# The closing order of two output projections, one W_out piece in another ring, and the memory projections' banks

## The chip, the cores and the metric

The kernel runs on one core of a Trainium2 chip. The metric is the device time of one execution in microseconds, here the median of several runs. TensorE does the matrix products and writes them to PSUM; VectorE, ScalarE and GpSimd (POOL) work on SBUF, the first two also on PSUM; SyncE issues the transfers.

## The reference

A trunk of two layers on x of 1024 tokens by 1024 channels, with 256 memory tokens. In each layer:

```python
h = x @ w_in                      # columns: main | memory queries | main gate | memory gate
y_main = main_fn(u_main)          # layer 0: causal pooling; layer 1: forgetting attention, 16 heads
y_mem  = memory_attention(q_mem, mem, w_mem_kv)      # 4 heads of 128 over 256 memory tokens
y = concat([y_main * silu(g_main), y_mem * silu(g_mem)]) @ w_out     # 1536 x 1024
x = layer_norm(ALPHA * x + y, ln_g, ln_b)
```

Memory attention first makes keys and values of the memory tokens: `mem @ w_mem_kv`, four heads of each. All of it is in float32.

## The kernel before, in words

**Products in three parts.** A float32 operand is split into a high half (a cast on ScalarE, L187) and a low half (a subtract on VectorE, or on POOL for some weights, L188, L198). One product of float32 numbers becomes three on TensorE (`three`, L217): high by high ("large", f32 in the profile) and two with a low half ("small", bf16). `grouped` (L222) puts the large ones ahead of the small ones, or behind them when it is `turned`.

**Slots.** Tiles come from rings by tag: `T` has 6 slots, `w` and `wl` 4 each (high and low halves of weights), `raw` 4 (weights as they arrive), `MK`, `Y`, `P`, `G` 4 each. A tile takes a slot of its tag that is free at that point of the compiled order, and its first writer waits for the last reader of what was there. PSUM's banks are tagged as well: `pj` 2, `L` 3, `T` 2, `O` 1. TensorE's instructions keep the order of the program (`manual_schedule`). Those of the other engines are put in order when the kernel is compiled, by what is ready and, among that, by the program's order; each engine then takes its queue in that order.

**Output projection** (`OutProj`, L432). The tokens go in four pairs of token tiles (sp = 0 to 3, two tiles `a` of 128 tokens). Each pair has four banks, `accs[a][nh]`, one for each token tile and half of the columns. The rows of W_out go in three chunks `c` of 512 rows, four row tiles `k` each, in the order c = 2, 0, 1. A chunk is 48 products of 512 columns (2 token tiles x 2 halves x 4 row tiles x 3). `products` (L474) issues them: all 16 large ones, then all 32 small ones (for c = 0 the other way round), each in the order token tile, half, row tile. So all four banks of a pair stay open into the small products of c = 1. For each chunk `rest` (L500) loads `src` and splits it (`hi_lo`, L517), which takes three slots of `T`: source, high, low.

**Norm** (L527). After c = 1 each token tile is normalised on VectorE: L537 takes up a bank (alpha times x plus the product), L538 its statistics, twice; L540 to L546 make the mean and the reciprocal root (with one square root on ScalarE, L542); L548 and L550 are the two passes over the 1024 columns, in halves for the very last tile; then the tile is stored (L551). In layer 0 the normalised tiles are also transposed on TensorE (L348) for layer 1; those of the last pair are put between layer 1's memory projections (L361).

**W_out.** Its 12 pieces (256 rows by 512 columns) are split ahead of use into whatever slots are free; `wtags` (L651 for layer 0) names the tag of each. Pieces 0 to 3 serve chunk 2, 4 to 7 chunk 0, 8 to 11 chunk 1; even ones are the first half of the columns. A piece in the weights' ring takes 2 slots of `w` and all 4 of `wl`.

**Memory keys and values** (`mem_kv`, L286). The memory rows are split into four tiles of `T`. `project` (L298) makes one head's keys or values: 24 products of 256 columns into a `pj` bank, with two pieces of weights (one low half on POOL and one on VectorE in layer 1). Keys are split from the bank into `MK` (L315); values are scaled first (`scaled_halves`, L327: a reduction and five short instructions on VectorE, then L339 on ScalarE and L340 on VectorE read the bank). In layer 0 keys and values of a head follow its queries (L364 to L370); in layer 1 all eight projections come first, keys then values, with the two transposes between, and then the queries' products (`slab`, L253, also into `pj`).

Of the kernel before, what the change touches and what calls it, by code (L numbers as in the profile page):

```python
# [18 lines left out]
P = 128  # L19
# [3 lines left out]
ST = S // P  # L23
NH = 512
HEADS = 16
MH = 4
NMEM = 256
# [72 lines left out]
def trunk_kernel(ctx, tc, x, xT, memT, win, wk, wv0, wv, wmk, wmv, wout, poolw, pscale, lng, lnb, bforget, out):  # L100
# [21 lines left out]
    def nm(tag):  # L122
        count[0] += 1
        return f"{tag}{count[0]}"

    def sb(shape, tag, bufs, dt=F32, where=None):
        return (where or pool).tile(shape, dt, tag=tag, name=nm(tag), bufs=bufs)

    def ps(shape, tag, bufs):
        return psum.tile(shape, F32, tag=tag, name=nm(tag), bufs=bufs)  # L130
# [4 lines left out]
    def T(shape=(P, S), dt=F32R):  # L135
        return sb(list(shape), "T", 6, dt)

    def MK(shape, dt=F32R):
        return sb(list(shape), "MK", 4, dt)

    def raw(shape):
        return sb(list(shape), "raw", 4)
# [8 lines left out]
    def cut(pair, *key):  # L151

        return type(pair)(t[key] for t in pair)

    def halved(make, shape):

        return make(list(shape)), duo(make([shape[0], 2, *shape[1:]], BF16))

    def in_place(make, shape):

        hi = make(list(shape))
        return hi, InPlace((make(list(shape), BF16), hi.bitcast(BF16)[..., 1::2]))
# [21 lines left out]
    def hi_lo(hi, lo, src, pinned=False, aside=False, by=nc.vector):  # L184

        pin = tc.keep_in_program_order if pinned else lambda ins: ins
        pin(nc.scalar.copy(hi, src))  # L187
        pin(by.tensor_tensor(lo[0], src, hi.bitcast(F32), ALU.subtract))  # L188
        if isinstance(lo, InPlace):
            return  # L190
        if pinned or aside:
            nc.gpsimd.tensor_scalar(lo[1], hi.bitcast(F32), 1.0, 1.0, ALU.mult, ALU.mult)  # L192
        else:
            nc.scalar.copy(lo[1], hi.bitcast(F32))
# [5 lines left out]
    def split_w(src_dram, shape, by=nc.vector):  # L200
        r = raw(shape)
        nc.sync.dma_start(r, src_dram)
        h, l = in_place(wt, shape)
        gp_hi_lo(h, l, r) if low[0] else hi_lo(h, l, r, by=by)
        return h, l
# [11 lines left out]
    def three(a, b):  # L217

        (ah, al), (bh, bl) = a, b
        return (ah, bh), (al[1], bl[0]), (al[0], bl[1])  # L220

    def grouped(triples, turned=False):  # L222


        large, small_ = [t[0] for t in triples], [m for t in triples for m in t[1:]]
        return small_ + large if turned else large + small_

    def mm3(acc, terms):

        for i, (a, b) in enumerate(terms):  # L230
            nc.tensor.matmul(acc, a, b, start=i == 0, stop=i == len(terms) - 1)  # L231
# [54 lines left out]
    def mem_kv(l):  # L286

        mh, ml = zip(*(halved(T, [P, 4, NMEM]) for _ in range(2)))
        for q in range(4):
            r = raw([P, 2, NMEM])  # L290
            nc.sync.dma_start(r, memT[:, 2 * q : 2 * q + 2, :])
            two = slice(2 * (q % 2), 2 * (q % 2) + 2)
            hi_lo(mh[q // 2][:, two, :], cut(ml[q // 2], slice(None), two), r)
        kh, kl = halved(MK, [P, MH, NMEM])

        turned = [False]

        def project(w_dram):  # L298

            acc = ps([P, NH], "pj", 2)[:, :NMEM]  # L300
            terms = []
            for pc in range(2):
                a, b = split_w(w_dram[pc], [P, 4, P], nc.gpsimd if l and not pc else nc.vector)
                terms += [
                    three((a[:, k, :], cut(b, slice(None), k)), (mh[pc][:, k, :], cut(ml[pc], slice(None), k))) for k in range(4)
                ]
            turned[0] = not turned[0]
            mm3(acc, grouped(terms, turned[0]))
            return acc

        two, v = (MK([P, MH, 2 * 2, P], F16) for _ in range(2))
        undo = const.tile([P, 8], F32, tag="undo", name=nm("undo"), bufs=1)[:, :MH]

        def keys(h):
            hi_lo(kh[:, h, :], cut(kl, slice(None), h), project(wmk[l, h]))  # L315

        def vals(h):
            scaled_halves(
                project(wmv[l, h]), [two[:, h, 2 * e : 2 * e + 2, :].rearrange("p m t -> p (m t)") for e in range(2)],
                undo[:, h : h + 1],  # L320
            )
            if h == MH - 1:
                nc.sync.dma_start_transpose(v.rearrange("p h b d -> p (h b) d"), two.rearrange("p h b t -> p (h b t)"))

        return (kh, kl, v, undo), keys, vals

    def scaled_halves(u, halves, un, by_tile=lambda t: t):  # L327

        m, e, sc = (tiny(1) for _ in range(3))
        nc.vector.tensor_reduce(m, u, AX.X, ALU.max, apply_absolute_value=True)
        nc.vector.tensor_scalar(m, m, 2.0 ** -100, None, ALU.max)
        nc.vector.tensor_scalar(e.bitcast(I32), m.bitcast(I32), 0x7F800000, None, ALU.bitwise_and)
        nc.vector.reciprocal(sc, e)
        nc.vector.tensor_scalar(sc, sc, 2.0 ** 14, None, ALU.mult)
        nc.vector.tensor_scalar(un, e, 2.0 ** -15 / PSCALE, None, ALU.mult)
        (hi, lo), u = halves, by_tile(u)
        nc.scalar.activation(hi, u, AF.Copy, scale=sc)  # L339
        nc.vector.scalar_tensor_tensor(lo, u, sc, hi, ALU.mult, ALU.subtract)  # L340
# [91 lines left out]
    class OutProj:  # L432
# [38 lines left out]
            accs = [ps([P, NH], *bank) for bank in turned[sp % len(turned)]]  # L471
            return accs[:2], accs[2:]

        def products(self, accs, c, yh, yl):  # L474
            terms = []
            for a in range(2):
                rows = slice(a * P, (a + 1) * P)
                for nh in range(2):
                    for k in range(4):
                        kt = 4 * c + k  # L480
                        w = tuple(part[kt % 2] for part in self.ws[nh][kt // 2])
                        terms.append([(accs[a][nh], x) for x in three((yh[:, k, rows], cut(yl, slice(None), k, rows)), w)])
            order = grouped(terms, c == 0)
            firsts, lasts = ({id(acc): j for j, (acc, _) in way} for way in (reversed(list(enumerate(order))), enumerate(order)))
            for j, (acc, (y, w)) in enumerate(order):
                nc.tensor.matmul(acc, y, w, start=c == 2 and j == firsts[id(acc)], stop=c == 1 and j == lasts[id(acc)])  # L486
                yield NH
# [12 lines left out]
        def rest(self, resid, XH, XL, dst):  # L500
            self.split(24)
            gb = []
            for v in (lng, lnb):
                t = sb([P, D], "P", 4)
                nc.sync.dma_start(t, v[self.l].partition_broadcast(P))
                gb.append(t)
            accs, turns = {}, []
            if self.accs:
                accs[0], order = self.accs, [(0, 0), (1, 2), (0, 1), (1, 0), (1, 1)]
            else:  # L510
                order = [(sp, c) for sp in range(2) for c in (2, 0, 1)]
            for sp, c in order + [(sp, c) for sp in range(2, ST // 2) for c in (2, 0, 1)]:
                if c == 2:
                    accs[sp] = self.open(sp)
                src, (yh, yl) = T([P, 4, 2 * P], F32), in_place(T, [P, 4, 2 * P])
                nc.sync.dma_start(src, self.yd[c, :, :, sp * 2 * P : (sp + 1) * 2 * P])
                hi_lo(yh, yl, src)  # L517
                for n, _ in enumerate(self.products(accs[sp], c, yh, yl)):
                    at = (sp, ((2, 0, 1).index(c) * 48 + n))
                    while turns and turns[0][0] <= at:  # L520
                        turns.pop(0)[1]()
                if c == 1:
                    made = norm(sp, accs.pop(sp), gb, resid, XH, XL, dst)
                    turns += [((sp + 1, n), turn) for n, turn in zip((44, 84), made)]
            return [turn for _, turn in turns]
# [66 lines left out]
    with tc.tile_pool(name="in0", bufs=1) as in0:  # L592
# [55 lines left out]
                    nc.vector.scalar_tensor_tensor(yn, acc, pschalf[:, f : f + 1], yn, ALU.mult, ALU.mult)  # L648
                nc.sync.dma_start(y0d[f // 4, :, f % 4, :], ys[d])

        wtags = [("B", 8)] * 4 + [("W", 4)] * 2 + [("MK", 4)] * 2 + [("Y", 4)] * 2 + [("PG", 0), ("w", 0)]  # L651
        out_proj = OutProj(0, w_slots(wtags, in0), y0d)
        order = ExitStack()
        order.enter_context(tc.manual_schedule(engines={PE}))
# [13 lines left out]
    with tc.tile_pool(name="in1", bufs=1) as in1:  # L668
# [390 lines left out]
        wtags = [("B", 10), ("V", 4), ("MK", 4)] + [("B", 10)] * 3 + [("w", 0), ("MK", 4), ("R", 2), ("V", 4), ("PG", 0), ("B", 10)]  # L1059
# [69 lines left out]
```

## Time and profile before

| | |
|---|---|
| median of 3 runs | 1225.47 us (1223.59 to 1226.15) |
| the profiled execution | 1221.52 us, its span 1219.8 us |
| TensorE busy | 1187.1 us, 97% of the span |
| VectorE, ScalarE, POOL busy | 786.8, 607.5, 201.7 us |
| granted TensorE clock, mean | 0.997 |
| layer 0's last product (L486) to the queries' first of layer 1 (L253) | about 461 to 489.76 us |
| last product of layer 1 starts | 1208.63 us |

Lines of the timeline give start and length in us, engine, line, operation, what is written and read, and how many were merged; in brackets the idle time of the engine before it and what ended it. A line of the waits gives the total, the number and the longest. A product's end is modelled: 0.27 us after its start for 256 columns and 0.38 for 512, while the next may start sooner. Names such as `wl` or `L` are the tags above. The share of busy time hardly tells anything here; what counts is where TensorE stands still.

### The profile page before, as it was taken

How to read it: one execution, taken by the hardware profiler on the slowest of the kernel's cores; microseconds unless marked ns; L12 is line 12 of the kernel's file. 1: busy time of each engine (PE TensorE's matmuls, PEld its weight loads, DVE VectorE, ACT ScalarE, POOL GpSimd, SP SyncE). 2: the span in 40 equal slices, each digit the busy share in tenths (PEclk: the TensorE clock that was granted, in tenths of full speed). 3: DMA queues.
4: the chain of work that ended last, by engine and by line, in shares of the span. 5: the costliest groups of instructions: out<-in, count | busy, mean ns of one | idle time of the engine just before them, and what ended most of it. 6: DMA issues, size and time to landing. Idle time of an engine off the chain costs nothing. (4 is left out here: it accounts for less than half of the span.)

```text
span 1219.8 us, 19568 instructions
## 1 busy us (share of the span) xinstructions
PE 1187.1 (97%) x6903; PEld 749.7 (61%) x7018; DVE 786.8 (64%) x1861; ACT 607.5 (50%) x1318; POOL 201.7 (17%) x312
## 2 busy tenths in 40 slices
PE   9999999999999998999999999999999999999996
PEld 4567665555556567557776666666666666655553
DVE  6544776375554459247645878777878878775653
ACT  6433654263431134257434777767766777673110
POOL 2000000000000004000003334333334324530000
PEclk9999999999999999999999999999999999999998
DMA  6332454242363325224618688769797999985430
GB/s 233 114 105 90 125 113 156 79 130 89 119 207 111 113 104 174 87 59 107 183 50 176 162 186 174 193 154 184 176 190 175 174 200 212 226 232 187 167 109 35
DMA packets 267410, 178.65 MB, mean 146 GB/s; under 512 B 212272, under 2 KB 225712, under 8 KB 267312
## 3 DMA queue, kind: packets, MB, share of 16 engines
q1 hardware_dynamic: 267312, 177.40, 55.5%
q8 instruction: 55, 0.90, 0.3%
q14 instruction: 43, 0.35, 0.1%
HBM read 94.97 MB, written 22.61 MB: 96 GB/s over the span
## 5 line engine op out<-in xcount | busy, mean ns | idle before, releaser
L253 PE MATMUL pj<-A,w 128*128 128x512 f32 (+1 forms) x1888 | 600.4, 399 | 3.5 <-ACT A L187 1.2
L253 PE MATMUL pj<-A,wl 128*128 128x512 bf16 x951 | 360.1, 380 | 4.3 <-issue 0.5
L253 PEld LDWEIGHTS pj<-A,w 128*128 128x128 f32 x976 | 180.9, 189 | 46.6 <-ACT A L187 2.2
L253 PEld LDWEIGHTS <-w 128*128 128x128 bf16 x992 | 95.8, 98 | 123.7 <-issue 36.3
L253 PEld LDWEIGHTS <-wl 128*128 128x128 bf16 x992 | 97.6, 98 | 94.2 <-issue 6.0
L880 ACT ACTIVATE T<-MK,s 128x512 f32<-128x512 f32 x192 | 111.0, 578 | 57.8 <-DVE s L872 36.1
L902 DVE SCALAR_TENSOR_TENSOR P<-T,s,P 128x512 f16<-128x512 f32 x192 | 111.8, 612 | 32.1 <-ACT P L901 30.5
L901 ACT ACTIVATE P<-T,s 128x512 f16<-128x512 f32 x192 | 102.7, 576 | 49.5 <-issue 27.4
L188 DVE TENSOR_TENSOR wl<-raw,w 128x512 bf16<-128x512 f32 x98 | 70.2, 721 | 84.7 <-ACT w L187 84.3
L486 PEld LDWEIGHTS <-T 128*128 128x128 bf16 x736 | 70.8, 98 | 86.6 <-issue 3.9
L187 ACT CAST w<-raw 128x512 fp32r<-128x512 f32 x106 | 64.7, 618 | 101.7 <-PE pj L253 67.0
L231 PE MATMUL L<-B,B 128*128 128x512 f32 (+3 forms) x384 | 110.7, 390 | 4.6 <-DVE s L872 4.4
L231 PEld LDWEIGHTS L<-B,B 128*128 128x128 f32 x384 | 70.6, 189 | 31.2 <-DVE s L872 12.1
L192 POOL TENSOR_SCALAR A<-A 128x512 bf16<-128x512 f32 (+1 forms) x20 | 16.8, 856 | 435.7 <-ACT A L187 435.7
L872 DVE CUSTOM_DVE_ANT_0 MK<-L,R 128x512 f32<-128x512 f32 (+3 forms) x128 | 72.5, 567 | 6.8 <-PE L L231 3.1
L864 POOL TENSOR_SCALAR_AFFINE_SELECT R<-R 128x128 f32<-128x128 f32 x128 | 41.5, 330 | 207.0 <-DVE s L872 112.0
L187 ACT CAST T<-T 128x1024 fp32r<-128x1024 f32 x23 | 24.1, 1046 | 95.0 <-DMA T<-y1d 50.5
L198 POOL TENSOR_TENSOR wl<-raw,w 128x512 bf16<-128x512 f32 x54 | 69.1, 1280 | 3.5
L188 DVE TENSOR_TENSOR T<-T,T 128x1024 bf16<-128x1024 f32 x23 | 29.0, 1261 | 41.1 <-ACT T L187 21.2
L197 POOL TENSOR_SCALAR w<-raw 128x512 fp32r<-128x512 f32 x54 | 34.3, 635 | 74.0 <-DMA B<-B 47.3
L231 PE MATMUL pj<-T,w 128*128 128x256 bf16 (+1 forms) x256 | 44.6, 281 | 1.8 <-DVE MK L340 1.2
L486 PE MATMUL L<-B,T 128*128 128x512 bf16 (+1 forms) x165 | 43.1, 389 | 0.2
(255 smaller groups left out, 1726.1 us busy)
## 6 DMA issues: line engine op xcount, KB each, us to landing
raw<-in_win_dram SPq DMA_DIRECT2D x96, 256.0 KB, 2.8
raw<-in_wout_dram SPq DMA_DIRECT2D x40, 256.0 KB, 2.8
B<-B SPq DMA_DIRECT2D x32, 256.0 KB, 4.8
R<-cumd SPq DMA_DIRECT2D x16, 512.0 KB, 4.4
y0d<-Y SPq DMA_DIRECT2D x12, 512.0 KB, 2.8
T<-y0d SPq DMA_DIRECT2D x12, 512.0 KB, 3.9
T<-y1d SPq DMA_DIRECT2D x11, 512.0 KB, 3.9
raw<-in_wmk_dram SPq DMA_DIRECT2D x16, 256.0 KB, 2.5
```

Of the source, the lines that this page charges most:

```text
L187: pin(nc.scalar.copy(hi, src))
L188: pin(by.tensor_tensor(lo[0], src, hi.bitcast(F32), ALU.subtract))
L197: nc.gpsimd.tensor_scalar(hi, src, 1.0, 1.0, ALU.mult, ALU.mult)
L198: nc.gpsimd.tensor_tensor(lo[0], src, hi.bitcast(F32), ALU.subtract)
L231: nc.tensor.matmul(acc, a, b, start=i == 0, stop=i == len(terms) - 1)
L253: nc.tensor.matmul(acc, a, b, start=start, stop=stop)
L486: nc.tensor.matmul(acc, y, w, start=c == 2 and j == firsts[id(acc)], stop=c == 1 and j == lasts[id(acc)])
L864: nc.gpsimd.affine_select(R[:, qs], R[:, qs], [[-1, P]], ALU.is_ge, -NEG, base=0, channel_multiplier=1).ins
L872: nc.vector.tensor_tensor_reduce(p[:, lo:up], lg, R[:, lo:up], 1.0, top, ALU.add, ALU.min, m[:, n : n + 1])
L880: nc.scalar.activation(e, p[:, lo:up], AF.Exp, bias=top, scale=-1.0, accum_out=sums[:, n, hd % 2, i : i + 1],)
L901: nc.scalar.activation(pair[:, lo:up], e, AF.Copy, scale=r)
L902: nc.vector.scalar_tensor_tensor(pair[:, L + lo : L + up], e, r, pair[:, lo:up], ALU.mult, ALU.subtract)
```

## The change

Three edits. First, for the last pair of token tiles (sp = 3) of each layer's output projection, the 96 products of c = 0 and c = 1 are issued together by a new function, `closing`, after c = 2: token tile 0's two banks first (16 large, 32 small), then token tile 1's first bank (16 small, 8 large), then its second (8 large, 16 small). The source and halves of c = 0 and c = 1 are both made before it. Second, in layer 0 the piece in the weights' ring is piece 6 (rows 256 to 511, first half of the columns) in place of piece 11; pieces 7 to 11 take the tags that 6 to 10 had. Third, `project` takes its bank from `pj` and `L` in turn, beginning with `pj`: in layer 0 keys in `pj` and values in `L`, in layer 1 first, third, fifth and seventh projection in `pj`.

```diff
-            acc = ps([P, NH], "pj", 2)[:, :NMEM]
+            acc = ps([P, NH], *(("pj", 2), ("L", 3))[turned[0]])[:, :NMEM]
...
-        def products(self, accs, c, yh, yl):
-            terms = []
+        def terms(self, accs, c, yh, yl):
+            terms = [], [], [], []
             for a in range(2):
                 rows = slice(a * P, (a + 1) * P)
                 for nh in range(2):
                     for k in range(4):
                         kt = 4 * c + k
                         w = tuple(part[kt % 2] for part in self.ws[nh][kt // 2])
-                        terms.append([(accs[a][nh], x) for x in three((yh[:, k, rows], cut(yl, slice(None), k, rows)), w)])
-            order = grouped(terms, c == 0)
+                        three_ = three((yh[:, k, rows], cut(yl, slice(None), k, rows)), w)
+                        terms[2 * a + nh].append([(accs[a][nh], x) for x in three_])
+            return terms
+
+        def products(self, accs, c, yh, yl):
+            return self.ordered(grouped(sum(self.terms(accs, c, yh, yl), []), c == 0), c)
+
+        def closing(self, accs, ys):
+            parts = [sum(two, []) for two in zip(*(self.terms(accs, c, yh, yl) for c, (yh, yl) in enumerate(ys)))]
+            return self.ordered(grouped(parts[0] + parts[1]) + grouped(parts[2], True) + grouped(parts[3]), 1)
+
+        def ordered(self, order, c):
...
+            kept = []
             for sp, c in order + [(sp, c) for sp in range(2, ST // 2) for c in (2, 0, 1)]:
...
                 hi_lo(yh, yl, src)
-                for n, _ in enumerate(self.products(accs[sp], c, yh, yl)):
-                    at = (sp, ((2, 0, 1).index(c) * 48 + n))
+                at_end = sp == ST // 2 - 1 and c != 2
+                kept += [(yh, yl)] if at_end else []
+                if at_end and c == 0:
+                    continue
+                for n, _ in enumerate(self.closing(accs[sp], kept) if at_end else self.products(accs[sp], c, yh, yl)):
+                    at = (sp, ((2, 0, 0 if at_end else 1).index(0 if at_end else c) * 48 + n))
...
-        wtags = [("B", 8)] * 4 + [("W", 4)] * 2 + [("MK", 4)] * 2 + [("Y", 4)] * 2 + [("PG", 0), ("w", 0)]
+        wtags = [("B", 8)] * 4 + [("W", 4)] * 2 + [("w", 0), ("MK", 4), ("MK", 4), ("Y", 4), ("Y", 4), ("PG", 0)]
```

## The prediction

> **What bounds the kernel now.** I read the page first, then TensorE's waits, then the timelines of three places.
>
> ```profile
> PE 1187.1 (97%) x6903; PEld 749.7 (61%) x7018; DVE 786.8 (64%) x1861; ACT 607.5 (50%) x1318; POOL 201.7 (17%) x312
> ```
>
> TensorE is busy nearly throughout, and the change leaves its 6903 products as they are. So a gain can come only from stretches in which TensorE stands still: a few waits, and the tail after its last product. The profiled run took 1221.52 us; the runs shown have a median of 1225.47, 3.95 above it. I take differences from the trace and apply them to the median.
>
> The waits of TensorE between 461 and 491 us, which is layer 1's memory projections (columns: waiter, releaser, us in total, times, longest):
>
> ```profile
> PE pj L231 <- DVE MK L340: 1.2, 1, 1.2
> PE pj L253 <- DVE MK L340: 0.9, 1, 0.9
> PE pj L231 <- DVE wl L188: 0.8, 1, 0.8
> PE pj L231 <- POOL wl L188: 0.7, 1, 0.7
> PE pj L231 <- DVE MK L188: 0.7, 1, 0.7
> ```
>
> Two are for the low halves of weights (wl), three for a pj bank that an eviction (L340 of values, L188 of keys) hasn't emptied. Ends of products are modelled, so the true loss is read from starts:
>
> ```profile
> 460.93 0.27 PE L231 MATMUL pj<-T,w 128*128 128x256 bf16 x1
> 461.90 0.28 PE L231 MATMUL pj<-T,wl 128*128 128x256 bf16 x1 [0.70 <-POOL wl L188]
> 462.02 0.27 PE L231 MATMUL pj<-T,w 128*128 128x256 bf16 x1
> ```
>
> Undisturbed, products of 256 columns start 0.11 to 0.12 apart; here 0.97, so 0.86 is lost where the table says 0.70. With 0.16 added to each, the five cost 4.3 + 0.8 = **5.1 us**: 1.8 on wl, 3.3 on banks.
>
> The tail, from the timeline of all engines:
>
> ```profile
> 1208.63 0.38 PE L486 MATMUL O<-B,T 128*128 128x512 bf16 x1
> ...
> 1210.04 0.68 DVE L537 SCALAR_TENSOR_TENSOR G<-G,O 128x512 f32<-128x512 f32 x1
> ...
> 1210.76 0.69 DVE L538 BATCH_NORM_STATS2 s<-G 128x6 f32<-128x512 f32 x1
> 1211.37 1.27 DVE L550 SCALAR_TENSOR_TENSOR G<-G,s,P 128x1024 f32<-128x1024 f32 x1
> 1212.55 0.20 DVE L540 BATCH_NORM_AGGREGATE s<-s 128x2 f32<-128x12 f32 x1
> ...
> 1214.92 1.42 DVE L550 SCALAR_TENSOR_TENSOR G<-G,s,P 128x512 f32<-128x512 f32 x2
> ```
>
> The last product ends at 1209.01, but VectorE takes up its bank (O) only at 1210.04, and L550 of 1.27 us, which belongs to token tile 6, stands ahead of tile 7's L540. VectorE is the bound of the last 10 us.
>
> **The change part by part.**
>
> *Token-tile order, layer 1.* The 96 products are the same; 32 are f32, 64 bf16:
>
> ```profile
> 1187.71 1.03 PE L486 MATMUL T<-B,T 128*128 128x512 bf16 x4
> 1188.57 1.03 PE L486 MATMUL T<-wl,T 128*128 128x512 bf16 x4
> ...
> 1196.01 0.62 PE L486 MATMUL T<-MK,T 128*128 128x512 f32 x2
> 1196.47 0.63 PE L486 MATMUL L<-B,T 128*128 128x512 f32 x2
> ```
>
> Starts are 0.23 apart for f32 and 0.215 for bf16. Tile 6's banks now close after 32 and 48 of the 96, the third after 72; 64 products and 48 remain, 10.4 us for tile 6's second bank instead of 3.4. Tile 6's normalisation (two each of L537 and L538, its L550 and as long an L548, and five short ones: some 6 us of VectorE) and the third bank's L537 and L538 lie wholly beside products. When O closes, VectorE is free: L537 at about 1209.05 instead of 1210.04, L538 0.72 later as now, L540 as soon as that has ended, at 1210.50 instead of 1212.55. What follows L540 holds tile 7's work alone and keeps its 3.79 us (1212.55 to 1216.34). **Tail: -2.05 us.** ScalarE's square roots wait for VectorE only.
>
> The new order needs the second chunk's operands (c = 1) at once, so I look at when they are ready:
>
> ```profile
> 1181.02 1.04 ACT L187 CAST T<-T 128x1024 fp32r<-128x1024 f32 x1 [5.02 <-DMA T<-y1d]
> 1187.70 1.23 DVE L188 TENSOR_TENSOR T<-T,T 128x1024 bf16<-128x1024 f32 x1 [1.99 <-PE O L486]
> ```
>
> That is the last cast of layer 1: the high half lies ready at 1182.1, 5.8 us before chunk 2's products end. The low half gets its slot as they end and is ready at 1188.9. The closing order first reads it after 16 f32 and 8 bf16 products, 5.4 us in. Cost 0, with 4 us of cover.
>
> *Layer 0's end: the weights' ring.* W_out's last piece holds all four wl slots to the last product; the weights of the first two memory projections wait for it:
>
> ```profile
> 460.54 2.54 POOL L188 TENSOR_TENSOR wl<-raw,w 128x512 bf16<-128x512 f32 x2 [11.05 <-PE L L486]
> 463.01 0.68 DVE L188 TENSOR_TENSOR wl<-raw,w 128x512 bf16<-128x512 f32 x1
> ```
>
> The piece now put there (rows of chunk 0, first half of the columns) is last read as wl at the 64th of the 96 and as w at the 72nd, so 24 to 32 products, 5.2 to 6.9 us, before the end. Two subtracts on POOL (2.54) and one on VectorE (0.68) fit. **wl: -1.8 us.** Tile 6's normalisation moves ahead of the end here too and takes some 5 us of VectorE off the first two projections.
>
> The price is in the T ring. Memory rows 4 to 7 wait for chunk 0's slots:
>
> ```profile
> 446.01 1.14 ACT L187 CAST T<-raw 128x512 fp32r<-128x512 f32 x2 [0.23 <-PE L L486]
> 450.64 1.14 ACT L194 CAST T<-T 128x512 bf16<-128x512 f32 x2 [1.94 <-PE L L486]
> 450.58 1.29 DVE L188 TENSOR_TENSOR T<-raw,T 128x512 bf16<-128x512 f32 x2 [1.05 <-PE L L486]
> ```
>
> Now chunk 0 is read up to the 88th product, so both slots come free about 459.4. Two casts and two copies (2.28) end at 461.7, the subtracts (1.29, from the first cast on) by 461.4. The first projection starts at 460.93 and reaches these rows after eight products, at 461.81. Cost 0 on this count; behind the two casts of a later weight (1.26 to 1.37) it is 1.3. I take 0, as every row fits, and keep 1.3 for the range.
>
> *W_out's earlier pieces.* Layer 0's first chunks show no wait for weights, and the last piece was ready 8 us early:
>
> ```profile
> 341.76 0.62 ACT L194 CAST wl<-w 128x512 bf16<-128x512 f32 x1
> 351.24 0.62 PE L486 MATMUL pj<-w,T 128*128 128x512 f32 x2
> ```
>
> The pieces change places among slots that come free between 323 and 334 us. Cost 0; what hides it is the 20 us of chunks 2 and 0.
>
> *Two kinds of banks.* Of layer 1's eight projections four go to L, which has three banks. A bank then has two projections' time to be emptied, not one. The slowest eviction is that of the second values, whose products end before the transposes that follow, and whose bank is read last by L340:
>
> ```profile
> 480.99 1.04 PE L348 MATMUL T<-ident,G 128*128 128x128 f32 x8
> 485.36 0.48 DVE L340 SCALAR_TENSOR_TENSOR MK<-pj,s,MK 128x256 f16<-128x256 f32 x1 [0.54 <-ACT MK L339]
> ```
>
> That is 4.85 us, and two projections take 5.3. **Banks: -3.3 us** at most. In layer 0 no projection waits for a bank, so 0; L is next used there only after all queries.
>
> What is late next is the weights. By rows of the stretch:
>
> ```profile
> 477.67 1.13 ACT L187 CAST w<-raw 128x512 fp32r<-128x512 f32 x2
> 478.36 1.28 POOL L188 TENSOR_TENSOR wl<-raw,w 128x512 bf16<-128x512 f32 x1 [1.28 <-ACT w L187]
> 478.83 1.36 DVE L188 TENSOR_TENSOR wl<-raw,w 128x512 bf16<-128x512 f32 x1
> 473.13 0.62 ACT L187 CAST w<-raw 128x512 fp32r<-128x512 f32 x1 [1.40 <-DMA raw<-in_wmv_dram]
> 484.85 0.47 ACT L339 ACTIVATE MK<-pj,s 128x256 f16<-128x256 f32 x1 [1.88 <-DVE s L336]
> ```
>
> From the first cast to both low halves is 2.5 us (477.67 to 480.19), and a projection lasts 24 x 0.11 = 2.64, so projection k+2 is ready 0.1 us before TensorE wants it, if nothing delays ScalarE. But ScalarE has stood 1.4 us for a weight's transfer and 1.9 us for VectorE's scale, and its queue is in order. Bounds: 0, if VectorE's freed 5 us pulls the chain ahead, to 3.3, if it swallows all that the banks give. I take 1.3, one such stall shown on TensorE.
>
> The VectorE subtract begun beside POOL's takes 1.36 and ends 0.55 after it; alone it takes 0.68 (463.01). Were it always 0.68, both halves would be ready at POOL's end, the slack would be 0.65, and I would book 0 for this term: 1218.3.
>
> The Trainium skill, page "SBUF — State Buffer", section "Who interferes with whom", says that a VectorE instruction with two SBUF inputs contends with a GpSimd instruction that reads SBUF, and that the loser fully blocks. By that rule the pair never runs side by side, here or after the change; the trace agrees (POOL ends at 479.64, VectorE 0.55 later). It speaks against the full gain, 1218.3, and for the sum below.
>
> **Sum:** -2.05 - 1.8 - 3.3 + 1.3 = **-5.9 us**: 1221.52 becomes 1215.6 for a profiled run, the median 1225.47 becomes **1219.6**.
>
> **Rivals.**
> 1. *Weights instead of banks.* TensorE reaches each values projection sooner and waits for wl. For: the 0.1 us of slack, VectorE's doubled subtract. Against: the rows are of a time when VectorE also had tile 6's and 7's normalisation. Gain 2.05 + 1.8 = 3.9: 1221.6.
> 2. *The memory stage gains nothing.* The T ring costs 1.3 and the weights' chain keeps its pace whenever it starts, since each raw slot is refilled only after a subtract. For: the wait of ScalarE for a transfer (473.13). Against: the first two weights are now split before the end. Gain 2.05: 1223.4.
> 3. *Slower.* ScalarE's queue puts the memory rows' casts, held by T slots until 459.4, ahead of tile 6's square root, and VectorE stands behind that. Before, VectorE took up this normalisation at
>
> ```profile
> 455.95 0.69 DVE L537 SCALAR_TENSOR_TENSOR G<-G,pj 128x512 f32<-128x512 f32 x1 [4.08 <-PE pj L486]
> ```
>
> and would now go on with it up to 3.5 us later, the weights' subtracts behind it. The whole stage moves by that and by the 1.3 of the T ring, and the gains on wl and banks are lost in it: +3.5 + 1.3 - 2.05 = +2.75, 1228.2, decided once block and ring cost over 2.05. Against: in the trace the order of casts follows the order in which slots came free.
> 4. *The change doesn't do what it says*: slots come from a free list, so wl may be taken otherwise, and tile 6's work may stand behind tile 7's. 1225.5.
>
> **How the numbers follow.** Forecast 0.57, rival 1 0.19, rival 2 0.12, rival 3 0.08, rival 4 0.04. The forecast's own range is 1218.3 (nothing lost) to 1222.2 (1.3 more for T, 1.3 more for weights). The range for 8 in 10 goes from 1217.5, the full 7.15 and 0.8 more for the spread of runs (1223.59 to 1226.15 before), to 1223.9, which takes in rival 2. A measurement of this kernel can tell about 0.2% (2.5 us) from no change. Faster by more than that, under 1223.0: the forecast, rival 1 and a quarter of rival 2, 0.79; within 0.2%: the rest of rival 2, rival 4, a quarter of rival 3, 0.15; slower: the rest of rival 3, 0.06.
>
> **What would show it.** Tail: L537 on O within 0.1 us of the last product, no L550 of 1024 columns behind it, 7.3 us from the last product's end to the last L550 become 5.3. wl: TensorE's waits at the first projection gone, POOL's pair of wl subtracts starting before the last product. Banks: no wait of L231 or L253 for L340 or MK L188; the queries' first product 28.8 us after the first projection's now, about 25 then. Wrong: waits for wl, w or T at those places, or a TensorE wait inside the 96 products.

## The result, and the profile after

The changed kernel takes 1214.38 us (median of 5, 1211.57 to 1216.94) where the kernel before, run beside it, takes 1223.59 (1221.66 to 1226.15): ratio 0.9919, 95% interval 0.9895 to 0.9942. Timed twice more it gave 0.9927 (0.9913 to 0.994) and 0.9921 (0.9909 to 0.9933). So it is faster, as forecast, but by some 9 us and not by 5.9, and below the range.

The profiled execution took 1214.61 us, its span 1212.9. The page's line of busy time:

```profile
PE 1185.1 (98%) x6902; PEld 748.8 (62%) x7018; DVE 789.8 (65%) x1861; ACT 607.9 (50%) x1318; POOL 202.6 (17%) x312
```

The work is the same; only time in which TensorE stood still has gone. Line numbers behind the changed functions are larger by 12 to 17: L498 was L486, L554 was L537, L557 was L540, L567 was L550.

The five largest entries in the list of TensorE's waits, over the whole execution:

```profile
PE L L231 <- DVE s L889: 4.4, 13, 0.6
PE pj L498 <- DVE G L284: 1.5, 1, 1.5
PE O L948 <- DMA T<-P: 1.4, 1, 1.4
PE idle L120 <- DVE warm L117: 1.3, 1, 1.3
PE pj L253 <- ACT A L187: 0.9, 1, 0.9
```

None is of the memory projections; their five waits are gone, and a list of that stretch alone is empty. The timeline of TensorE there:

```profile
459.45 1.03 PE L498 MATMUL L<-G,T 128*128 128x512 bf16 x4
460.31 0.27 PE L231 MATMUL pj<-T,w 128*128 128x256 bf16 x1
460.42 0.27 PE L231 MATMUL pj<-T,wl 128*128 128x256 bf16 x1
...
483.65 1.17 PE L253 MATMUL pj<-A,w 128*128 128x512 f32 x4
```

The second product now follows the first by 0.11 us (0.97 before), and the queries begin 23.34 us after the first projection. Below I call this distance "the stage": 28.83 us in the trace of before (460.93 to 489.76). That is 5.49 less.

The tail:

```profile
1203.12 1.03 PE L498 MATMUL O<-B,T 128*128 128x512 bf16 x4
1204.18 0.69 DVE L554 SCALAR_TENSOR_TENSOR G<-G,O 128x512 f32<-128x512 f32 x1 [3.88 <-PE O L498]
1204.91 0.69 DVE L555 BATCH_NORM_STATS2 s<-G 128x6 f32<-128x512 f32 x1
1205.63 0.21 DVE L557 BATCH_NORM_AGGREGATE s<-s 128x2 f32<-128x12 f32 x1
...
1208.01 1.41 DVE L567 SCALAR_TENSOR_TENSOR G<-G,s,P 128x512 f32<-128x512 f32 x2
```

VectorE has been idle for 3.88 us when the last bank closes at 1204.15, takes it up at once, and has only tile 7's work left. From the start of the last product (1203.77) to the end of the span it is 9.13 us; before 11.17 (1208.63 to 1219.8). That is 2.04 less, and I call this distance "the tail" (the span is shown to 0.1 us, so tails are good to 0.05).

Stage and tail make -7.53 us; the spans differ by 6.9. The stage begins 0.62 us sooner than before (460.31 and 460.93), and from its end to the last product it is 1.25 us longer (720.12 and 718.87). The change leaves that long stretch as it was, and in the two later traces of the changed kernel it took 718.8 and 717.8 us, so this is scatter. The times differ by more, 9.2. Two questions follow: why the 1.3 us that I held back for the weights did not appear, and where the rest of the difference is.

### The profile page after: what moved, and what is told of

Its sections match the earlier page's. It is cut to its first block, busy times and chain, and to the rows that moved or that the text cites. A ratio compares the mean times of both kernels' runs of the same rounds, so it can differ in the third digit from the quotient of the medians.

```text
span 1212.9 us, 19574 instructions
## 1 busy us (share of the span) xinstructions
PE 1185.1 (98%) x6902; PEld 748.8 (62%) x7018; DVE 789.8 (65%) x1861; ACT 607.9 (50%) x1318; POOL 202.6 (17%) x312
## 5 line engine op out<-in xcount | busy, mean ns | idle before, releaser
L188 DVE TENSOR_TENSOR wl<-raw,w 128x512 bf16<-128x512 f32 x98 | 72.0, 739 | 82.5 <-ACT w L187 80.3
L498 PEld LDWEIGHTS <-T 128*128 128x128 bf16 x736 | 70.6, 98 | 86.4 <-issue 4.4
L188 DVE TENSOR_TENSOR T<-T,T 128x1024 bf16<-128x1024 f32 x23 | 29.0, 1261 | 42.5 <-ACT T L187 22.5
L498 PE MATMUL L<-B,T 128*128 128x512 bf16 (+1 forms) x165 | 43.3, 391 | 0.2
L889 DVE CUSTOM_DVE_ANT_0 MK<-L,R,s 128x512 f32<-128x512 f32 (+1 forms) x64 | 37.2, 581 | 7.5 <-POOL R L881 4.1
```

The costliest lines, as they stand in the source:

```text
L889: nc.vector.tensor_tensor_reduce(p[:, lo:up], lg, R[:, lo:up], 1.0, top, ALU.add, ALU.min, m[:, n : n + 1])
```

## The experiments

Theory A was at first: each part of the change removes its own wait, and nothing takes its place. Theory B: the parts depend on each other, since the weights' chain takes part of the gain unless the token-tile order in layer 0 relieves VectorE.

**Each part alone.** Layer 1's order alone (`closing` only where `self.l == 1`):

```diff
-                at_end = sp == ST // 2 - 1 and c != 2
+                at_end = sp == ST // 2 - 1 and c != 2 and self.l == 1
```

with the old bank line and the old `wtags`.

> The token-tile order in layer 1 alone; W_out's pieces and the projections' banks as before, layer 0 as before. Theory A (each part removes its own wait and nothing takes its place): from the start of the last product to the end of the span 11.2 us become 9.1, the stage from the first memory projection of layer 1 to its queries' first product stays at 28.8; time -2.05 us, ratio 0.998. Rival (the new order puts a wait for the operands of chunk 1 between the products): the gain is smaller and TensorE shows an idle stretch after chunk 2 of the last pair.

Measured: tail 9.13, the whole 2.04, with no wait between the 96 products. Ratio 0.9964 (0.9952 to 0.9977), more than the tail explains; and the stage, whose code is that of before, took 30.09 us and not 28.83. I come back to both.

Banks alone (the changed line of `project` in the kernel before):

> Two kinds of banks alone, the rest as before. The stage from layer 1's first memory projection to the queries' first product takes 28.83 us before. Theory A (the weights always had some 1 us of slack): 28.83 - 3.3 = 25.5, no wait of TensorE for weights beyond the two of before; ratio 0.9973. Rival B (the prediction's term of 1.3 us: the weights' chain takes back part of the gain unless VectorE is relieved of tile 6's normalisation): 26.8, with new waits for wl or w.

Measured: stage 26.75, 2.08 less than in the trace of before, ratio 0.9961 (0.9948 to 0.9973). The figure is rival B's. TensorE's timeline, and ScalarE's:

```profile
478.88 0.87 PE L231 MATMUL L<-T,w 128*128 128x256 f32 x5 [0.89 <-ACT w L187]
```

```profile
478.21 0.62 ACT L187 CAST w<-raw 128x512 fp32r<-128x512 f32 x1 [2.34 <-DMA raw<-in_wmv_dram]
```

No bank holds TensorE up any more. The two waits for wl at the first projection are there as before, and there is a new one at the sixth, for a weight whose transfer ScalarE awaits for 2.34 us. That isn't B's reason, which was VectorE: the transfers issued between 473.0 and 474.3 us took 4.3 to 4.5 us to land here, and 2.7 to 2.9 in the trace of before. So B's figure was met by luck. How much the landing of these transfers moves the stage by itself is seen below, in the traces of the kernel before.

The ring alone (the changed `wtags` in the kernel before):

> The other W_out piece in the weights' ring alone, order and banks as before. Without the closing order that piece is free 48 products before the end. Theory A: both waits for wl at the first projection vanish, 28.83 - 1.8 = 27.0; ratio 0.9985. Rival B: POOL's halves come in time, but VectorE, still busy with tile 6 and 7, splits its half late: only some 0.9 us are gained, 27.9.

Measured: stage 27.92, 0.91 less, ratio 0.9977 (0.9966 to 0.9987). Again it is B's figure, though not quite its place. TensorE and VectorE:

```profile
468.68 0.28 PE L231 MATMUL pj<-T,wl 128*128 128x256 bf16 x1 [1.47 <-DVE s L545]
```

```profile
466.10 1.73 DVE L548 SCALAR_TENSOR_TENSOR G<-G,s,P 128x512 f32<-128x512 f32 x1
467.76 0.26 DVE L544 TENSOR_SCALAR s<-s,s 128x1 f32<-128x1 f32 x1
467.94 0.68 DVE L188 TENSOR_TENSOR wl<-raw,w 128x512 bf16<-128x512 f32 x1
```

The first projection waits for nothing. The third now waits 1.47 us for its second low half, which stands on VectorE behind tile 7's L548. So VectorE's queue decides, with the normalisation ahead. One thing makes it worse: this L548 took 1.73 us, where the same half took 0.72 in the trace of before. It ran beside a subtract on POOL and ended 0.54 us after that, as VectorE's subtract in the prediction ended 0.55 us after POOL's:

```profile
466.02 1.27 POOL L188 TENSOR_TENSOR wl<-raw,w 128x512 bf16<-128x512 f32 x1 [0.46 <-ACT w L187]
```

The whole change beside them:

> The changed kernel once more, beside its parts on one chip. Theory A: what the two traces show, 5.5 us in the memory stage and 2.05 in the tail, is all: -7.5 us, ratio 0.9939. Rival C: something outside of these two places gives another 1.7 us (the first comparison said -9.2): ratio 0.992 again, and a third place in the trace is shorter than before.

Measured: stage 23.34, tail 9.16, ratio 0.9927. No third place is shorter. Against the one trace of before, banks (2.08) and ring (0.91) alone sum to 2.99, and all together give 5.49. Either the order in layer 0 brings the difference, or it is scatter of single traces; both are looked at below.

**Parts together.** Order in layer 0 alone (`self.l == 0` in the line above):

> The token-tile order in layer 0 alone. The weights' ring is held to the last product as before, and one kind of bank. Theory A (the order frees VectorE of tile 6's normalisation, and that pays only where wl and banks no longer stand in the way): the two waits for wl at the first projection stay (1.8 us), so do those for banks; the stage takes 28.3 to 28.8, the tail as before, ratio 0.9995. Rival (the T ring's price: memory rows 4 to 7 split after the 88th product): a wait for T or for ScalarE at the ninth product of the first projection, the stage 29.5 or more.

Measured: stage 29.05, ratio 0.9995 (0.9986 to 1.0004). TensorE's waits:

```profile
462.61 0.28 PE L231 MATMUL pj<-T,wl 128*128 128x256 bf16 x1 [1.11 <-POOL wl L188]
468.64 0.28 PE L231 MATMUL pj<-T,wl 128*128 128x256 bf16 x1 [1.22 <-DVE wl L188]
486.41 1.34 PE L231 MATMUL pj<-T,w 128*128 128x256 f32 x9 [1.19 <-DVE MK L340]
490.28 1.20 PE L253 MATMUL pj<-A,w 128*128 128x512 f32 x4 [0.89 <-DVE MK L340]
```

By itself it gains nothing, as A and B have it: wl and the banks stand in the way. The second of these waits is at the 18th product of the second projection, the first that reads VectorE's low half there. Nothing waits at the ninth product of the first projection, so the T ring brings no wait of its own. But the first wait for wl is 1.11 us instead of 0.70: POOL's subtract took 1.72 us here and 1.31 before, and beside it VectorE subtracted the memory rows that the T ring had held back (from 460.14 us on).

All but the order in layer 0 (`self.l == 1` in the changed kernel):

> Ring and banks of the change, token-tile order in layer 1 only. Theory A: without the relief of VectorE the two bring no more than their sum alone, 28.83 - 0.91 - 2.08 = 25.8, with waits for weights at the third projection or later; tail 9.1; ratio 0.9959. Rival (the stage's waits are simply those five and each part removes its own): 23.7, ratio 0.994.

Measured: stage 24.98, ratio 0.9939 (0.9924 to 0.9954). That is 1.64 more than with it, between the two expectations (25.8 and 23.7). There is one wait left:

```profile
468.61 0.28 PE L231 MATMUL pj<-T,wl 128*128 128x256 bf16 x1 [1.47 <-DVE s L562]
```

It is the wait of the ring alone, at the third projection, and on VectorE too the same normalisation stands ahead. With ring and banks the order in layer 0 is worth these 1.64 us, and 0 by itself, by one trace each.

All but the banks, and all but the ring:

> The whole change but one kind of bank (pj) as before. Theory A: waits for banks of 3.3 us come back, and nothing else: 23.34 + 3.3 = 26.6; ratio 0.9955. Rival (with VectorE relieved the evictions come sooner and the banks suffice): 24 to 25.

Measured: stage 26.28, ratio 0.995 (0.9935 to 0.9965); the waits for L340 are back, the one for MK L188 is not.

```profile
482.80 1.34 PE L231 MATMUL pj<-T,w 128*128 128x256 f32 x9 [1.50 <-DVE MK L340]
486.67 1.20 PE L253 MATMUL pj<-A,w 128*128 128x512 f32 x4 [0.89 <-DVE MK L340]
```

> The whole change but W_out's last piece in the weights' ring as before. Theory A: the two waits for wl come back, 23.34 + 1.8 = 25.1, as the later projections keep their slack; ratio 0.9945. Rival (the late first weights delay the whole chain, each raw slot being refilled after a subtract): 26.5 or more, with waits for weights from the third projection on.

Measured: stage 26.01, between the two; ratio 0.9948 (0.9926 to 0.9971).

```profile
462.04 0.28 PE L231 MATMUL pj<-T,wl 128*128 128x256 bf16 x1 [1.11 <-POOL wl L188]
467.98 0.28 PE L231 MATMUL L<-T,wl 128*128 128x256 bf16 x1 [1.00 <-DVE wl L188]
```

Besides the first wait for wl there is one at the second projection's 18th product, for VectorE's half, as with the order alone. That the raw slots are refilled only after the first weights' subtracts would explain it, and wasn't tried by itself. So all eight combinations of the three parts in layer 0's end and layer 1's start have been measured:

| stage, us | neither bank nor ring | banks | ring | both |
|---|---|---|---|---|
| order of before in layer 0 | 28.83 | 26.75 | 27.92 | 24.98 |
| token-tile order in layer 0 | 29.05 | 26.01 | 26.28 | 23.34 |

Each cell is one trace but the last, which came out the same each time; the first is the lowest of five (below). So a small difference between two cells means something only where a named wait comes or goes with it.

**Is it VectorE's relief?** In the changed kernel four redundant instructions give VectorE its load back behind the last product:

```diff
                 nc.vector.bn_stats(stats[:, 6 * nh : 6 * nh + 6], zn)
+                for _ in range(4 if XH is not None and s == ST - 1 and nh else 0):
+                    nc.vector.bn_stats(stats[:, 6 * nh : 6 * nh + 6], zn)
```

> The changed kernel with four more statistics instructions (0.69 us each, the same values written again) on VectorE after layer 0's last bank, so that about 2.8 us of VectorE come back behind the last product. Theory A (the order's share of 1.6 us is VectorE's relief): the wait for VectorE's weights at the third projection comes back, the stage takes 24.5 to 26. Rival (the share comes from something else that the order moves, such as the earlier split of the first weights): 23.3 to 23.7.

Measured: stage 24.80, 1.46 more. (The single execution took 1214.0 us; the scatter of times hides a difference of this size.)

```profile
474.88 0.28 PE L231 MATMUL pj<-T,wl 128*128 128x256 bf16 x1 [1.28 <-DVE wl L188]
```

```profile
462.39 2.15 DVE L557 BATCH_NORM_STATS2 s<-G 128x6 f32<-128x512 f32 x3
...
464.78 0.68 DVE L557 BATCH_NORM_STATS2 s<-G 128x6 f32<-128x512 f32 x1
465.38 0.67 DVE L188 TENSOR_TENSOR wl<-raw,w 128x512 bf16<-128x512 f32 x1
```

The load brings back a wait for VectorE's half of a weight, of the size that the order had saved, but at the fifth projection and not the third. That VectorE's load behind the last product makes this wait is shown; that the order helps by nothing else is not.

**How much slack had the weights?** Both low halves on POOL:

```diff
-                a, b = split_w(w_dram[pc], [P, 4, P], nc.gpsimd if l and not pc else nc.vector)
+                a, b = split_w(w_dram[pc], [P, 4, P], nc.gpsimd if l else nc.vector)
```

> The changed kernel with both low halves of each memory weight in layer 1 made by POOL, one after the other (1.28 us each), none by VectorE. A weight is then ready about 3.2 us after its first cast instead of 2.5. Theory A (its second half is read only from the ninth product on, so that the slack was about 1 us, not the 0.1 that the prediction counted): the stage takes 23.3 to 24.3. Rival (slack 0.1): every second projection waits 0.6 us or more, the stage takes 26 or more.

Measured: stage 23.33, no wait. POOL works in long runs:

```profile
463.12 8.49 POOL L188 TENSOR_TENSOR wl<-raw,w 128x512 bf16<-128x512 f32 x6 [4.46 <-ACT w L187]
471.58 1.19 POOL L192 TENSOR_SCALAR A<-A 128x512 bf16<-128x512 f32 x2
472.75 6.22 POOL L188 TENSOR_TENSOR wl<-raw,w 128x512 bf16<-128x512 f32 x5
```

For the last four projections it is now 3.6 to 3.8 us from the first cast to the second low half, and 2.5 in the changed kernel. So the weights take 1.1 to 1.3 us longer, more than the 0.7 expected. At the sixth projection the second low half is ready 0.92 us after the projection has begun:

```profile
473.99 1.29 POOL L188 TENSOR_TENSOR wl<-raw,w 128x512 bf16<-128x512 f32 x1
474.36 1.12 PE L231 MATMUL L<-T,w 128*128 128x256 f32 x8
```

TensorE doesn't wait even there, because this projection has its large products first and reads that half only at the 18th, 2.0 us in. With 0.1 us of slack it would have waited. In the changed kernel itself the second low half is always ready before its projection begins, at the third by the least, 0.29 us:

```profile
464.24 1.20 DVE L188 TENSOR_TENSOR wl<-raw,w 128x512 bf16<-128x512 f32 x1
465.73 0.27 PE L231 MATMUL pj<-T,w 128*128 128x256 bf16 x1
```

**A further version.** Layer 1's first chunk waits 1.5 us for a pj bank, so other banks were tried:

```diff
-            turned = ((l, l, pj, pj), (t, t, l, o)) if self.l else ...
+            turned = ((l, l, t, t), (pj, pj, l, o)) if self.l else ...
```

> The changed kernel; in layer 1's output projection the first and third pair use banks L, L, T, T and the second and fourth pj, pj, L, O (before: L, L, pj, pj and T, T, L, O). Theory A: the wait of the first chunk for a pj bank that the last gate's eviction (L284) holds, 1.5 us in the waits, is gone, -1.6 us against the changed kernel: ratio to before 0.9915. Rival: T is held as long by the last heads' probabilities, and the wait only changes its name: 0.993.

Measured: ratio 0.9932 (0.9909 to 0.9955), no better than the change. Two of TensorE's waits:

```profile
PE T L498 <- DVE P L919: 1.4, 1, 1.4
...
PE L L498 <- ACT T L187: 1.1, 1, 1.1
```

The wait has changed its name, as the rival said.

**Where the rest of the difference is.** The kernel before, once more:

> The kernel before, a second trace. Theory A (the stage of the memory projections varies between executions, with the landing of the weights' transfers, and the trace of before was a short one): the stage takes between 28.8 and 30.1, as the run with only layer 1's order changed had 30.1 in this untouched stage. Rival: 28.8 again, and the spread of the times lies elsewhere.

Measured: stage 29.31. And the controls, with the order in layer 1 alone and the whole change once more:

> The kernel before, timed against itself. Theory A (the traces account for the change, and times scatter by some 0.2%): ratio 1.000, within 0.9985 to 1.0015, the untouched stages as in the other traces. Rival (a kernel set beside the one before comes out faster by 1 to 3 us whatever it is): ratio 0.9975 to 0.999, and the earlier ratios all contain that.

Measured: ratio 0.9995 (0.9985 to 1.0006), stage 29.19. So the comparison shows no bias of more than about 0.1%.

> The order in layer 1 alone, timed once more. It measured 0.9964 where its trace shows 2.04 us, 0.9983. Theory A: 0.998, the first figure having been at the low end of its scatter. Rival C (the order saves another 2 us in executions that no trace has shown): 0.9965 again, and a stage other than the tail shorter than in every trace of before.

Measured: ratio 0.9983 (0.9972 to 0.9993), just the 2.04 us of its tail (9.09); the 0.9964 of the first time was scatter. Its stage, untouched, took 31.48:

```profile
479.04 2.32 PE L231 MATMUL pj<-T,w 128*128 128x256 f32 x9 [2.39 <-DVE MK L188]
```

```profile
477.30 0.62 ACT L187 CAST w<-raw 128x512 fp32r<-128x512 f32 x1 [2.54 <-DMA raw<-in_wmv_dram]
477.83 0.36 ACT L187 CAST MK<-pj 128x256 fp32r<-128x256 f32 x1
```

ScalarE stands 2.54 us for a weight's transfer; behind that cast in its queue is the one that empties a pj bank, and TensorE waits 2.39 us for the bank. In the trace of before the same cast stood 0.89 us and TensorE 0.7. So the wait for MK L188 is a transfer's lateness, handed on through ScalarE's queue, and it differs from execution to execution: in four of the five traces with the stage as before the transfers issued around 473 us took 2.8, 3.4, 4.2 and 4.7 us to land, and TensorE waited 0.65, 1.12, 1.90 and 2.39. In the fifth (29.19) it didn't wait there at all, but 0.89 us at the third projection behind tile 7's normalisation, the place where the ring alone waits too.

> The whole change a third time, beside the two controls. Theory A: 0.993, the stage of the memory projections 23.3 and the tail 9.1 once more. Rival: 0.9915 or less.

Measured: stage 23.34, tail 9.10, ratio 0.9921.

With the stage as before there are five traces: 28.83, 29.19, 29.31, 30.09 and 31.48, on average 29.78. The changed stage was 23.34, 23.34 and 23.34, and 23.34 and 23.33 in the two kernels that alter something beside it. The average gain is 6.44 in the stage and 2.05 in the tail, 8.5 us, or 0.993 of the 1222.74 us that the kernel before took in the last comparison. That lies in all three intervals. No further effect is needed; that none below 1 us exists isn't shown. One figure doesn't fit as well: banks alone, timed in the comparison that gave the 0.9964, came out 4.8 us faster, and their trace shows 3.0 against the average. It wasn't timed again.

Against the average, the parts alone gain 3.0 (banks), 1.9 (ring) and 0.7 (order in layer 0), 5.6 of the 6.44 that they gain together. By the times they gain 4.8, 2.8 and 0.6, together 8.2 us, and the whole change, timed beside the first two, gains 6.9 without its tail. So the shortfall of 2.99 against 5.49 came mostly from the short trace of before and the late landing with banks alone. That the parts depend on each other is shown by the waits, not by such sums.

## Why the prediction was wrong, point by point

- **Tail, -2.05 us: right.** Measured -2.04, and alone at its full size. L537 (now L554) starts 0.03 us after the last product, as foreseen.
- **Operands of chunk 1 and W_out's earlier pieces at 0: right.** There is no wait between the 96 products in any trace of either layer.
- **T ring at 0: right for the whole change.** The first projection passes its ninth product without a wait. Where piece 11 stays in the weights' ring and the order in layer 0 is the new one, the memory rows' subtracts run beside POOL's, and the first wait for wl is 0.4 us longer.
- **wl, -1.8 us, and banks, -3.3 us: near in size in their own trace, one booked in the wrong place.** Together 5.1 was forecast; it was 5.49 by the same pair of traces, of which 1.84 at wl in the first projection, 0.18 at the third (a pause too short for the list), and 3.47 at the banks. By the average of five traces it was 6.44: the sum was made against one execution, and its stage was the shortest of the five. The wait for MK L188, taken as a constant 0.7 + 0.16 of a bank, is a late transfer. With banks alone such a transfer still held TensorE, at a weight (0.89); with piece 6 in the weights' ring that wait is in no trace, with banks or without. The room for wl was larger than reckoned, too: piece 6 is read as wl up to the 56th product and as w up to the 68th, not the 64th and 72nd.
- **Weights, +1.3 us: the step that failed.** "Projection k+2 is ready 0.1 us before TensorE wants it." The 2.5 us from first cast to both low halves are right, but they end with VectorE's half, which belongs to the projection's second four row tiles. It is read first by the tenth product, 1.0 us in, where the small products come first, and by the 18th, 2.0 us in, where the large ones do. Nor did the count have the two groups of transposes (0.87 us each) that stand between some projections. In the changed kernel the halves of the third to the eighth projection were ready 0.3 to 1.3 us before their projection began, so the slack to the first reading was 1.3 us or more, and the term was 0. With both halves on POOL, which makes them 1.1 to 1.3 us later, it was 0 as well. Two waits of this kind do exist in parts of the change: a late transfer at the sixth projection with banks alone (0.89), and VectorE's half at the third with ring and banks (1.47). The second goes with the order in layer 0 and comes back, at the fifth, when VectorE is loaded again. The prediction named that relief as the lower bound of this term, 0 to 3.3, and then took 1.3. It booked one part of the change a cost that another part removes.
- **The time.** 1219.6 was forecast and 1214.38 measured, 5.2 less. Of these 1.9 are the start, 1225.47 of three runs where the comparison has 1223.59 (and the last one, of 23, 1222.74). The gain was 9.2 instead of 5.9: 1.3 of the difference is the term for the weights, 0.4 the waits in the trace used, 0.95 that this trace was a short one, and the remaining 0.7 is within the scatter. Without the weights' term the forecast would have been 1218.3, still too high.
- **Rivals.** The first, weights instead of banks, is nearest to what the parts alone do, not the whole. None of the others occurred.

## What to carry to other kernels

When several edits serve one stage, price them together: ask for each cost of one whether another takes it away, as the order in layer 0 takes away the 1.47 us that ring and banks leave. Follow the named waits to see it; sums of single trials can mislead, as 2.99 against 5.49 did here, when each trial is one trace and the trace of before varies by 2.65 us. A wait that comes from a transfer through an in-order queue is not one number; look at several executions before summing against one, and count as gain also that it ends. And read slack from the product that uses the late half, not from the first product of its group.

## What was not expected of the hardware

The eight projections took the same 23.34 us, to 0.01, in five traces once nothing held TensorE, while the same stage before spread over 2.65 us. Its transfers did land unevenly in both: from issue to landing the weights took 2.4 to 4.7 us in the run whose stage was 31.48, and 2.4 to 3.8 in the changed kernel. In another trace of the change, with other banks in layer 1's output projection, they took up to 4.4 us, and ScalarE awaited none of them. Two kinds of banks alone don't give that: there a transfer of 4.4 us held TensorE. In all traces with piece 6 in the weights' ring ScalarE's longest wait for a weight's transfer in the stage was at most 1.2 us and no wait of TensorE followed from it; in those without, ScalarE's longest was 0.7 to 2.5 us. That the ring's earlier first subtracts, and with them earlier transfers, are the reason is argued from the program, not shown by a run of its own.
